# RMSNorm and matmul on one core: three more loads of sixteen tiles, squares nearer to their use, first casts in pieces

## Chip, core and metric

The kernel runs on one core of a Trainium2 chip. The metric is the device time of one execution in microseconds; the kernel before takes 209.28 us, the median of 7 runs (208.76 to 209.69). The engines of the core are named PE (matmul), ACT (ScalarE), DVE (VectorE), POOL (GpSimd) and SP (SyncE, which here only issues transfers). Sixteen DMA engines move the data.

## The reference

```python
batch, seq, dim, out_dim = 16, 1024, 512, 768
def reference(x, gamma, weight, eps):
    rms = np.sqrt(np.mean(x ** 2, axis=-1, keepdims=True) + eps)
    x_norm = x / rms * gamma
    return np.matmul(x_norm, weight).astype(np.float32)
```

All arrays are float32. There are 16,384 rows of x (33.5 MB), and as many rows of 768 results (50.3 MB).

## The kernel before

A tile is 128 rows of x; there are NT = 128 tiles, and NP = 64 pairs of tiles. The division by the rms is a scaling of a row, so it is done after the matmul, when a tile's sums leave PSUM; gamma is multiplied into the weights once, at the start.

**A tile's way.** A load brings rows of x into `xt`, two buffers of XG = 16 tiles. POOL casts them to bf16 (`cast`, L184 and L187). PE transposes a tile in two words of 128x128 float32, each of which holds two bf16 numbers (`transpose_word`, L225 and L229), and DVE copies the result from PSUM to `xT` (`evac`, L234 and L238). The last four tiles of each later group of sixteen go another way: POOL casts them at once into `xq` (`cast_quad`, L256 and L259), and DVE transposes 32x32 blocks, 16 instructions for a quad, three a turn (`move_quad`, L272, issued at L270). Then PE multiplies, four steps of 128 features, each with 512 and with 256 columns of the weights (`matmuls`, L305, instructions at L299), into one of three accumulators in PSUM. The even tile of a pair is scaled out of PSUM by ACT (L278), the odd one by DVE (L280), into `ot`. SP stores eight tiles at a time (L292), fewer at the start and the end.

**The scale.** ACT squares a tile and sums along the row in one instruction (`square`, L191 and L195, into `ssq`); `root` (L198) takes the root for several tiles on ACT (L200, into `rms`) and the reciprocal on DVE (L202, into `rstd`). For pairs 0 to 4 the squares and roots stand one pair ahead (`norms`). Pairs from 5 on follow the tables `NORM_GROUPS` and `norm_turns` (L211 to L213): in turn j the squares of pair j + 4 from turn 7 on, catching up in turns 5 and 6 with two pairs each, and a root for four pairs at a time, which stands with its reciprocal ahead of the turn's matmuls.

**Loads.** `x_first` and `x_size` (L137) say how tiles are loaded: group 0 in stretches of 2, 2, 4 and 8 tiles, groups 1, 5, 6 and 7 in two of 8, groups 2, 3 and 4 in one of 16. Within a group from 1 on, partition p holds sixteen neighbouring rows, so a load of 16 tiles moves 32 KB a partition in one piece, and one of 8 moves 16 KB. `load_until` (L180, called at L405) issues the loads of a group in turns 7, 15, 23 and so on: group g + 2 goes into the buffer of group g, and waits until all squares and casts that read the cells it overwrites are done. Groups 0 and 1 are loaded ahead of everything.

**The order of work** is written out by hand. The loop at L404 runs over the pairs j; one round is called a turn here. A turn lists, in this order: loads, casts (L406 to L411), quad cast or moves, squares and roots (L416 to L419), and then the matmuls of tiles 2j and 2j + 1. Between their steps `feeder` (L324) puts the transposes of pair j + 2, if it isn't of a quad. `Order.emit` then gives every engine its own instructions in that order, with a wait only where data or a buffer needs it. Each engine works through its list in order, and so does SP: a store that waits for its tiles holds up the load behind it.

The casts of a later group stand so: tiles 0 to 7 of it in turn 8g - 4 (one cast of eight), tiles 8 to 11 in turn 8g - 2, tiles 12 to 15 in turn 8g - 1 (the quad). Pair 8g, the first of a group, is transposed in turn 8g - 2.

Of the kernel before, what the change touches and what calls it, by code (L numbers as in the profile page):

```python
# [100 lines left out]
def kernel(  # L101
# [9 lines left out]
    PE, DVE, ACT, POOL, SP = nc.tensor, nc.vector, nc.scalar, nc.gpsimd, nc.sync  # L111
    order = Order(tc)

    def run(engine, issue, reads=(), writes=()):
        order.add(1, engine, issue, reads, writes)

    x = x.flatten_outer_dims()
    out = out.flatten_outer_dims()
# [4 lines left out]
    NP = NT // 2  # L123
    XG, OG = 16, 8
    AHEAD = 20

    def stretches(group, parts):
        first, size, i = {}, {}, 0
        for g in range(NT // group):
            for n in parts.get(g, [group]):  # L130
                for t in range(i, i + n):
                    first[t], size[t] = i, n
                i += n
        return first, size

    last = NT // OG - 1
    x_first, x_size = stretches(XG, {0: [2, 2, 4, 8], **{g: [8, 8] for g in (1, 5, 6, 7)}})  # L137
    o_first, o_size = stretches(OG, {0: [1, 1, 2, 4], last - 1: [4, 4], last: [4, 2, 2]})

    def rows(ap, i, n):  # L140
# [3 lines left out]
    def sb(name, shape, dtype):  # L144
        return nc.alloc_sbuf_tensor(name, shape, dtype).ap()
# [16 lines left out]
    rms = sb("rms", [P, NT], F32)  # L162
    rstd = sb("rstd", [P, NT], F32)
# [4 lines left out]
    def cells(name, slot, i, n=1):  # L168
        return [(name, slot, t) for t in range(i, i + n)]

    def x_of(i, n=1):
        return xt[i // XG % 2][:, i % XG:i % XG + n, :], cells("x", i // XG % 2, i % XG, n)
# [7 lines left out]
    def load_until(i):  # L180
        while starts and starts[0] < i:
            load(starts.pop(0))

    def cast(i, n=1):  # L184
        src, of = x_of(i, n)
        s = i // 8 % 2
        run(POOL, lambda: POOL.tensor_copy(out=xb[s][:, i % 8:i % 8 + n, :], in_=src), of, cells("xb", s, i % 8, n))  # L187
# [3 lines left out]
    def square(i):  # L191
        src, of = x_of(i)
        j = squares[0] % 2
        squares[0] += 1
        run(ACT, lambda: ACT.activation(out=jk[j], in_=src[:, 0, :], func=AF.Square, accum_out=ssq[:, i:i + 1]),  # L195
            of, [("jk", j), ("ssq", i)])

    def root(i, n):  # L198
        s = slice(i, i + n)
        run(ACT, lambda: ACT.activation(out=rms[:, s], in_=ssq[:, s], func=AF.Sqrt, scale=1.0 / D, bias=eps_sb),  # L200
            [("ssq", t) for t in range(i, i + n)] + ["eps"], [("rms", i)])
        run(DVE, lambda: DVE.reciprocal(out=rstd[:, s], in_=rms[:, s]), [("rms", i)],  # L202
            [("rstd", t) for t in range(i, i + n)])

    def norms(i, n):
        for t in range(n):
            square(i + t)
        root(i, n)


    NORM_GROUPS = [(5, 2), (7, 4)] + [(f, 4) for f in range(11, NP - 5, 4)] + [(NP - 5, 5)]  # L211
    norm_end = {f + s - 1: (2 * f, 2 * s) for f, s in NORM_GROUPS}
    norm_turns = {3: [5], 4: [6], 5: [7, 8], 6: [9, 10], **{j: [j + 4] for j in range(7, NP - 6)}, NP - 6: [NP - 2, NP - 1]}  # L213

    def norms_of_group(j):
        square(2 * j)
        square(2 * j + 1)
        if j in norm_end:
            root(*norm_end[j])

    def bank(j, t):

# [30 lines left out]
    def quad_of(j):  # L253
        return j // 2 if (2 * j) % XG >= XG - 4 and 2 * j >= XG else None

    def cast_quad(q):  # L256
        src, of = x_of(4 * q, 4)
        s = 4 * q // XG % 2
        run(POOL, lambda: POOL.tensor_copy(out=xq[s], in_=src), of, [("xq", s)])  # L259
        for t in range(4):  # L260
            xT_of[4 * q + t] = (xTq[s][:, t], ("xTq", s))
        words = xq[s].rearrange("p t d -> p (t d)").bitcast(F32).rearrange("p (a w) -> p a w", w=P)
        turned = xTq[s].rearrange("p t h m c -> p (t h m c)").bitcast(F32).rearrange("p (a m) -> p a m", m=P)
        for tokens in range(0, P, B):
            for features in range(0, P, B):
                quad_moves.append((turned[features:features + B, :, tokens:tokens + B],
                                   words[tokens:tokens + B, :, features:features + B], s))
# [4 lines left out]
    def move_quad(n):  # L272
        for _ in range(min(n, len(quad_moves))):
            move(*quad_moves.pop(0))

    def scale(engine, dst, src, r, reads, writes):
        if engine is ACT:
            run(ACT, lambda: ACT.mul(out=dst, in_=src, mul=r), reads, writes)  # L278
        else:
            run(DVE, lambda: DVE.tensor_single_scalar(out=dst, in_=src, scalar=r, op=mybir.AluOpType.mult), reads, writes)  # L280
# [3 lines left out]
    def accumulator():  # L284
        return next(turns) % 3

    def store(i):
        first, n = o_first[i], o_size[i]
        s = first // OG % 3
        if i == first + n - 1:  # L290
            src = ot[s][:, first % OG:first % OG + n, :]
            order.transfer(SP, lambda: SP.dma_start(out=rows(out, first, n), in_=src), reads=cells("ot", s, first % OG, n))  # L292
# [12 lines left out]
    def matmuls(i, a, ks, feed=None):  # L305
        block, cell = xT_of[i]
        for k in ks:
            lhsT = block[:, k // 2, :, k % 2]
            hold(lhsT, cell)
            for half, lo, hi in ((0, 0, WIDE), (1, WIDE, O)):  # L310
                product(ops[a][:, lo:hi], lhsT, w_bf[:, k, lo:hi], k == 0, k == K - 1,
                        [cell, ("w", k, half)], [("ops", a, half)])
            if feed:
                feed()

    def finish_tile(i, a, engine):
        s = i // OG % 3

        before = [("ot", s, i % OG - 1)] if i == o_first[i] + o_size[i] - 1 else []
        scale(engine, ot[s][:, i % OG, :], ops[a][:, :O], rstd[:, i:i + 1],  # L320
              [("ops", a, 0), ("ops", a, 1), ("rstd", i)] + before, [("ot", s, i % OG)])
        store(i)

    def feeder(pairs, gaps, alone=False):  # L324
        queue = [(j, t, h) for j in pairs for t in range(2) for h in range(2)]
        calls = iter(gaps)

        def feed():
            for _ in range(next(calls)):
                j, t, h = queue.pop(0)  # L330
                transpose_word(j, t, h)
                if alone and h == 1:
                    evac(j, t, 1)
                elif (t, h) == (1, 1):
                    evac(j)
        return feed
# [67 lines left out]
    for j in range(1, NP):  # L404
        load_until((2 * j + AHEAD + XG - 1) // XG * XG)  # L405
        if j in (1, 2):  # L406
            cast(4 * j + 4, 4)
        elif j % 8 == 4 and j + 4 < NP:
            cast(2 * j + 8, 8)
        elif j % 8 == 6 and j + 2 < NP:  # L410
            cast(2 * j + 12, 4)  # L411
        if (2 * j + 2) % XG == 0 and 2 * j + 2 < NT:
            cast_quad((2 * j + 2 + XG - 4) // 4)
        elif 2 * j >= XG:
            move_quad(3)
        if j < 4:  # L416
            norms(2 * j + 2, 2)
        for pair in norm_turns.get(j, []):
            norms_of_group(pair)  # L419
        if j < 3:  # L420
            feed = feeder([j + 1], mid if j == 1 else one, alone=j == 1)
        elif j == 3:
            feed = feeder([4, 5], both)
        elif j + 2 < NP and quad_of(j + 2) is None:
            feed = feeder([j + 2], two)
        else:
            feed = None
        for i, engine in ((2 * j, ACT), (2 * j + 1, DVE)):
            a = accumulator()
            matmuls(i, a, range(K), feed)  # L430
            finish_tile(i, a, engine)


    with tc.tile_critical():  # L434
# [45 lines left out]
```

## Time and profile before

| | |
|---|---|
| median of 7 runs | 209.28 us (208.76 to 209.69) |
| the profiled execution: its time, its span | 209.27 us, 207.5 us |
| PE busy | 192.8 us, 93% |
| DVE busy | 149.3 us, 72% |
| ACT busy | 144.5 us, 70% |
| POOL busy | 59.8 us, 29% |
| the DMA queue of loads and stores | 85.46 MB, 97.3% of the time of 16 engines |
| matmuls of tiles (L299), mean | 325 ns |
| transposes (L229), mean | 274 ns |
| squares (L195), 128 of them, mean | 619 ns |
| roots (L200), 20 of them, mean | 300 ns |
| reciprocals (L202), 20 of them, mean | 192 ns |
| cast of 8 tiles | 3.60 us |
| cast of 4 tiles | 1.89 us |
| cast of 2 tiles | 1.04 us |
| load of 16 tiles, issue to landing, median of 3 | 22.1 us |
| load of 8 tiles, issue to landing, median of 9 | 21.6 us |

The span runs from the first to the last instruction of one profiled execution; the time of that execution is 1.8 us longer. Busy time counts the instructions' own durations, without waits. PE overlaps its instructions, so its share says more than it is used. A load's time to landing holds the time that it waits behind earlier transfers.

### The profile page before, as it was taken

How to read it: one execution, taken by the hardware profiler on the slowest of the kernel's cores; microseconds unless marked ns; L12 is line 12 of the kernel's file. 1: busy time of each engine (PE TensorE's matmuls, PEld its weight loads, DVE VectorE, ACT ScalarE, POOL GpSimd, SP SyncE). 2: the span in 40 equal slices, each digit the busy share in tenths (PEclk: the TensorE clock that was granted, in tenths of full speed). 3: DMA queues.
4: the chain of work that ended last, by engine and by line, in shares of the span. 5: the costliest groups of instructions: out<-in, count | busy, mean ns of one | idle time of the engine just before them, and what ended most of it. 6: DMA issues, size and time to landing. Idle time of an engine off the chain costs nothing.

```text
span 207.5 us, 2761 instructions
## 1 busy us (share of the span) xinstructions
PE 192.8 (93%) x1212; PEld 72.3 (35%) x717; DVE 149.3 (72%) x255; ACT 144.5 (70%) x343; POOL 59.8 (29%) x34
## 2 busy tenths in 40 slices
PE   7789999999999999999999999999999999999910
PEld 1234444433334334432443334343334333432300
DVE  0455647998589957998579966999579975999310
ACT  4698897777768596856877686777777687763300
POOL 3247651019200390006700670006600373000000
PEclk9999999999999999999999999999999999999995
DMA  6999999999999999999999999999999999999992
GB/s 244 419 434 436 347 398 451 423 422 441 426 434 455 393 434 450 420 426 433 420 426 423 423 445 425 415 431 428 444 425 407 441 433 449 417 426 419 424 406 91
DMA packets 5632, 85.62 MB, mean 413 GB/s; under 512 B 626, under 2 KB 628, under 8 KB 1780
## 3 DMA queue, kind: packets, MB, share of 16 engines
q1 hardware_dynamic: 5616, 85.46, 97.3%
q8 instruction: 7, 0.11, 0.2%
q14 instruction: 5, 0.04, 0.0%
q10 hardware_dynamic: 4, 0.00, 0.0%
HBM read 35.13 MB, written 50.33 MB: 412 GB/s over the span
## 4 chain that ended last, share of the span: by engine, by line
PE 71%; DMA 16%; DVE 5%; issue 2%; SPq 1%; ACT 1%; POOL 1%; ACTq 0%
PE ps L299 62%; DMA xt<-in_x_dram 16%; PE ps L229 8%; DVE ot L280 2%; DVE xTq L270 2%; DVE xT L238 1%; POOL xb L187 1%; ACT jk L195 0%; SPq L344 0%; SPq L176 0%; ACT ot L278 0%; SPq L292 0%; DVE rstd L202 0%; SPq L475 0%; ACTq L93 0%
## 5 line engine op out<-in xcount | busy, mean ns | idle before, releaser
L299 PE MATMUL ps<-w_bf,xT 128*128 128x256 bf16 (+1 forms) x783 | 145.0, 325 | 2.3 <-DVE w_bf L280 1.0
L278 ACT ACTIVATE ot<-ps,rstd 128x768 f32<-128x768 f32 x64 | 57.5, 898 | 42.7 <-PE ps L299 41.1
L195 ACT ACTIVATE jk<-xt 128x512 bf16<-128x512 f32 x128 | 78.8, 619 | 6.7 <-DMA xt<-in_x_dram 6.6
L187 POOL CAST xb<-xt 128x2048 bf16<-128x2048 f32 (+3 forms) x21 | 46.2, 2218 | 112.2 <-DMA xt<-in_x_dram 107.9
L280 DVE TENSOR_SCALAR ot<-ps,rstd 128x768 f32<-128x768 f32 x64 | 64.8, 1013 | 8.9 <-PE ps L299 8.2
L295 PEld LDWEIGHTS <-xT 128*128 128x128 bf16 x400 | 39.2, 98 | 60.0 <-issue 51.9
L229 PE MATMUL ps<-ident_f,xb 128*128 128x128 f32 x200 | 53.9, 274 | 0.9 <-POOL xb L187 0.9
L238 DVE COPY xT<-ps 128x1024 bf16<-128x1024 bf16 (+1 forms) x53 | 34.5, 653 | 24.6 <-PE ps L229 22.9
L270 DVE STREAM_TRANSPOSE xTq<-xq 32x256 f32<-32x256 f32 x112 | 48.7, 435 | 3.4
L229 PEld LDWEIGHTS ps<-ident_f,xb 128*128 128x128 f32 x200 | 28.1, 142 | 46.3 <-issue 43.2
L299 PE MATMUL ps<-w_bf,xTq 128*128 128x256 bf16 (+1 forms) x217 | 41.8, 324 | 0.4
L195 ACT ACTIVATION_READ_ACCUMULATOR jk<-xt 128x1 f32 x128 | 24.3, 190 | 0.0
L295 PEld LDWEIGHTS <-xTq 128*128 128x128 bf16 x112 | 10.9, 98 | 14.5 <-issue 14.5
L259 POOL CAST xq<-xt 128x2048 bf16<-128x2048 f32 x7 | 13.3, 1893 | 0.0
L202 DVE RECIPROCAL rstd<-rms 128x8 f32<-128x8 f32 (+3 forms) x20 | 3.8, 192 | 7.5 <-ACT rms L200 7.3
L200 ACT ACTIVATE rms<-ssq,eps_sb 128x8 f32<-128x8 f32 (+3 forms) x20 | 6.0, 300 | 0.6
L299 PE MATMUL ps<-warm 128*128 128x512 bf16 x10 | 4.3, 571 | 1.4 <-DVE eps_sb L353 1.4
L278 ACT ACTIVATE w_bf<-w_f,g_sb 128x768 bf16<-128x768 f32 x2 | 1.9, 935 | 1.4 <-DMA w_f<-in_weight_dram 1.4
L376 DVE COPY g_sb<-ps 128x4 f32<-128x4 f32 x1 | 0.2, 162 | 3.2 <-PE ps L370 3.2
L340 ACT ACT_TABLE_LOAD x1 | 1.3, 1283 | 1.5 <-SPq L434 1.5
L280 DVE TENSOR_SCALAR w_bf<-w_f,g_sb 128x512 bf16<-128x512 f32 (+2 forms) x3 | 1.4, 482 | 0.8 <-DMA w_f<-in_weight_dram 0.8
L370 PEld LDWEIGHTS ps<-ident_f,g_row 2*128 2x128 f32 x2 | 0.3, 201 | 2.6 <-issue 2.6
(10 smaller groups left out, 1.9 us busy)
## 6 DMA issues: line engine op xcount, KB each, us to landing
out_dram<-ot SPq DMA_DIRECT2D x13, 3072.0 KB, 17.1
xt<-in_x_dram SPq DMA_DIRECT2D x9, 2048.0 KB, 21.6
xt<-in_x_dram SPq DMA_DIRECT2D x3, 4096.0 KB, 22.1
out_dram<-ot SPq DMA_DIRECT2D x4, 1536.0 KB, 11.8
out_dram<-ot SPq DMA_DIRECT2D x3, 768.0 KB, 8.5
w_f<-in_weight_dram SPq DMA_DIRECT2D x2, 768.0 KB, 5.4
xt<-in_x_dram SPq DMA_DIRECT2D x2, 512.0 KB, 5.1
xt<-in_x_dram SPq DMA_DIRECT2D x1, 1024.0 KB, 9.0
```

The costliest lines, as they stand in the source:

```text
L187: run(POOL, lambda: POOL.tensor_copy(out=xb[s][:, i % 8:i % 8 + n, :], in_=src), of, cells("xb", s, i % 8, n))
L195: run(ACT, lambda: ACT.activation(out=jk[j], in_=src[:, 0, :], func=AF.Square, accum_out=ssq[:, i:i + 1]), of, [("jk", j), ("ssq", i)])
L200: run(ACT, lambda: ACT.activation(out=rms[:, s], in_=ssq[:, s], func=AF.Sqrt, scale=1.0 / D, bias=eps_sb), [("ssq", t) for t in range(i, i ...
L202: run(DVE, lambda: DVE.reciprocal(out=rstd[:, s], in_=rms[:, s]), [("rms", i)], [("rstd", t) for t in range(i, i + n)])
L229: run(PE, lambda: PE.transpose(out=tp[b][:, t, h, :], in_=words[:, lo:lo + P], identity=ident_f), cells("xb", s, j % 4 * 2 + t) + ["ident" ...
L238: run(DVE, lambda: DVE.tensor_copy(out=dst[:, t:t + n, :], in_=src[:, t:t + n, :]), [("tp", b)], cells("xT", j % 4, t, n))
L259: run(POOL, lambda: POOL.tensor_copy(out=xq[s], in_=src), of, [("xq", s)])
L270: run(DVE, lambda: DVE.transpose(out=dst, in_=src), [("xq", s)], [("xTq", s)])
L278: run(ACT, lambda: ACT.mul(out=dst, in_=src, mul=r), reads, writes)
L280: run(DVE, lambda: DVE.tensor_single_scalar(out=dst, in_=src, scalar=r, op=mybir.AluOpType.mult), reads, writes)
L295: run(PE, lambda: PE.ldweights(lhsT), [cell])
L299: run(PE, lambda: PE.add_instruction(mybir.InstMatmult(name=nc.get_next_instruction_name(), engine=mybir.EngineType.PE, ins=[PE.lower_ap(r ...
```

## The change

- Groups 1, 5 and 6 (tiles 16 to 31 and 80 to 111) are loaded in one transfer of 4 MB each instead of two of 2 MB. Group 7 keeps its two halves.
- The tables of squares and roots go. In turn j, from 3 on, the squares of pair j + 2 are taken, and in every odd turn the root for two pairs (four tiles): pairs j + 1 and j + 2. Turn 3 takes one for pair 5 alone. Where a turn's squares read a tile of a new group, that is in turn 8g - 2 instead of 8g - 4.
- The reciprocal of such a root is put at the end of its turn on DVE, after the scale of tile 2j + 1; it used to stand ahead of the turn's matmuls.
- The cast of eight tiles in turn 8g - 4 becomes three: two, two and four tiles.

```diff
--- before.py
+++ after.py
@@ -134,7 +134,7 @@
         return first, size
 
     last = NT // OG - 1
-    x_first, x_size = stretches(XG, {0: [2, 2, 4, 8], **{g: [8, 8] for g in (1, 5, 6, 7)}})
+    x_first, x_size = stretches(XG, {0: [2, 2, 4, 8], **{g: [8, 8] for g in (7,)}})
     o_first, o_size = stretches(OG, {0: [1, 1, 2, 4], last - 1: [4, 4], last: [4, 2, 2]})
 
     def rows(ap, i, n):
@@ -195,12 +195,15 @@
         run(ACT, lambda: ACT.activation(out=jk[j], in_=src[:, 0, :], func=AF.Square, accum_out=ssq[:, i:i + 1]),
             of, [("jk", j), ("ssq", i)])
 
-    def root(i, n):
+    def root(i, n, later=None):
         s = slice(i, i + n)
         run(ACT, lambda: ACT.activation(out=rms[:, s], in_=ssq[:, s], func=AF.Sqrt, scale=1.0 / D, bias=eps_sb),
             [("ssq", t) for t in range(i, i + n)] + ["eps"], [("rms", i)])
-        run(DVE, lambda: DVE.reciprocal(out=rstd[:, s], in_=rms[:, s]), [("rms", i)],
-            [("rstd", t) for t in range(i, i + n)])
+
+        def invert():
+            run(DVE, lambda: DVE.reciprocal(out=rstd[:, s], in_=rms[:, s]), [("rms", i)],
+                [("rstd", t) for t in range(i, i + n)])
+        invert() if later is None else later.append(invert)
 
     def norms(i, n):
         for t in range(n):
@@ -208,15 +211,13 @@
         root(i, n)
 
 
-    NORM_GROUPS = [(5, 2), (7, 4)] + [(f, 4) for f in range(11, NP - 5, 4)] + [(NP - 5, 5)]
-    norm_end = {f + s - 1: (2 * f, 2 * s) for f, s in NORM_GROUPS}
-    norm_turns = {3: [5], 4: [6], 5: [7, 8], 6: [9, 10], **{j: [j + 4] for j in range(7, NP - 6)}, NP - 6: [NP - 2, NP - 1]}
-
-    def norms_of_group(j):
+    def norms_of_pair(j, later):
         square(2 * j)
         square(2 * j + 1)
-        if j in norm_end:
-            root(*norm_end[j])
+        if j == 5:
+            root(10, 2, later)
+        elif j % 2 == 1:
+            root(2 * j - 2, 4, later)
 
     def bank(j, t):
 
@@ -406,7 +407,9 @@
         if j in (1, 2):
             cast(4 * j + 4, 4)
         elif j % 8 == 4 and j + 4 < NP:
-            cast(2 * j + 8, 8)
+            cast(2 * j + 8, 2)
+            cast(2 * j + 10, 2)
+            cast(2 * j + 12, 4)
         elif j % 8 == 6 and j + 2 < NP:
             cast(2 * j + 12, 4)
         if (2 * j + 2) % XG == 0 and 2 * j + 2 < NT:
@@ -415,8 +418,9 @@
             move_quad(3)
         if j < 4:
             norms(2 * j + 2, 2)
-        for pair in norm_turns.get(j, []):
-            norms_of_group(pair)
+        later = []
+        if 3 <= j < NP - 2:
+            norms_of_pair(j + 2, later)
         if j < 3:
             feed = feeder([j + 1], mid if j == 1 else one, alone=j == 1)
         elif j == 3:
@@ -429,6 +433,8 @@
             a = accumulator()
             matmuls(i, a, range(K), feed)
             finish_tile(i, a, engine)
+        for invert in later:
+            invert()
 
 
     with tc.tile_critical():
```

## The prediction

> **What bounds the kernel now.** I read the page's slices first, then its DMA queues, then the windows, the waits of the SP queue, and last the timelines of PE, GpSimd and SP around the places the change touches. The slices (forty equal parts of the span; tenths busy):
>
> ```profile
> PE   7789999999999999999999999999999999999910
> DMA  6999999999999999999999999999999999999992
> GB/s 244 419 434 436 347 398 451 423 422 441 426 434 455 393 434 450 420 426 433 420 426 423 423 445 425 415 431 428 444 425 407 441 433 449 417 426 419 424 406 91
> ```
>
> Two resources look full at once. The windows of 23.5 us, one group of sixteen tiles each (columns: window, length, busy time of PE, weight loads, DVE, ACT, POOL with counts, clock, DMA share, GB/s), say the same in the middle of the run:
>
> ```profile
> 50.00:73.50 23.50, 23.34 (x151) 8.92 (x89) 19.15 (x33) 17.05 (x41) 5.92 (x3) 1.00 1.00 427
> 144.00:167.50 23.50, 23.34 (x151) 8.87 (x88) 19.16 (x33) 17.45 (x42) 6.90 (x3) 1.00 1.00 427
> ```
>
> Which one sets the end is read from the tail. Part 3 of the page and the end of the timeline:
>
> ```profile
> q1 hardware_dynamic: 5616, 85.46, 97.3%
> q8 instruction: 7, 0.11, 0.2%
> ```
> ```profile
> 196.21 3.20 SPq L292 DMA_DIRECT2D out_dram<-ot  x2
> 197.77 1.02 DVE L280 TENSOR_SCALAR ot<-ps,rstd 128x768 f32<-128x768 f32 x1 [1.58 <-PE ps L299]
> ```
> ```profile
> SPq L475 <- DMA out_dram<-ot: 7.1, 1, 7.1
> ```
>
> PE is done at 197.74, the last scale at 198.79, the last store is issued by 199.41, and then SP waits 7.1 us for it. That store is 768 KB, 1.8 us of work at 427 GB/s; the rest is queue. The records of single DMA packets make it plain: the fastest of the sixteen engines finishes its last packet at 202.2, the slowest at 206.1, and the slowest runs 6 KB packets back to back (234 ns each) right up to there. So the end is the slowest DMA engine's total work, and that engine would reach the last store's eight packets (8 x 0.234 = 1.9 us) only at about 204.2, while the store's data first move at 200.3. PE and everything behind it has some 3.9 us to spare. The lead of the fastest engine over the slowest grows from 0.6 us at 21 us to 3.5 us at 144 us.
>
> **What the Trainium skill says.** "DMA: Bandwidth & Descriptors", section on queues, rings and completion order: every DMA is split over up to sixteen engines and each consumes its ring in order; the section on the semaphore's 16 adds that a transfer has landed only when every engine has posted. The trace agrees: for tiles 88 to 95 the engines finish between 116.62 and 119.77, and the load counts as landed at 120.12. Its section on bandwidth gives 425 GB/s for a 16 MB load and a ceiling of 435; the windows show 427. "Runtime: NRT & Kernel Launch", section on instruction fetch, says that instructions are refilled by DMA in 16 KiB blocks, at a cost mostly hidden. The trace has seven such packets on queue 8, nearly 1 us each; with engines that are never idle, each delays the engine that carries it.
>
> **The change, part by part.**
>
> *Loads.* Three pairs of 2 MB loads become three 4 MB loads: 256 packets of 16 KB become 128 of 32 KB per group. Median packet durations are 611 ns and 1213 ns, so a merged pair saves 2 x 611 - 1213 = 9 ns. Each engine carries 8 per group: 8 x 9 = 72 ns, and one completion write of 9 ns; over three groups 3 x 81 = 0.24 us. Measured over whole groups it is less: the fastest engine takes 9.73, 9.75 and 9.78 us for groups 5, 6 and 7 (halves), and 9.80, 9.69 and 9.73 us for groups 2, 3 and 4 (whole), 9.75 against 9.74. Bounds 0 and -0.24; I take -0.15.
>
> *The same, for PE.* Tile 16's transposes can start only when all sixteen tiles have landed. GpSimd and PE before:
>
> ```profile
> 21.75 3.60 POOL L187 CAST xb<-xt 128x4096 bf16<-128x4096 f32 x1 [1.23 <-DMA xt<-in_x_dram]
> 28.31 1.89 POOL L187 CAST xb<-xt 128x2048 bf16<-128x2048 f32 x1 [2.96 <-PE ps L299]
> ```
> ```profile
> 28.34 0.27 PE L229 MATMUL ps<-ident_f,xb 128*128 128x128 f32 x1
> ```
>
> The second cast starts when the second half has landed (28.19 by its semaphore; "PE" as releaser is misread). The new cast of two tiles takes 1.04 us (the 128x1024 row at 9.39 us), so tiles 16 and 17 are ready at 29.35 and PE, which had transposed the first at 28.34 (turn j=6), stalls about 1.1 us. Pair 9's cast ends at 30.4, before its turn at 31.4 plus the stall. Had the cast stayed at eight tiles, the stall would have been 3.6; the split removes 2.56. For group 5 the whole load lands at 120.12; its cast ends at 121.3, and PE's first transposition there is at 122.43: covered. Group 6: 144.83, 146.0, and 145.85 plus the 1.1 already lost: covered. PE ends about 198.6 + (0 to 0.5), inside the 3.9 us. Without that cover the price is the full 1.1.
>
> *Who waits for a late PE.* Stores. The tightest place, in SP's timeline:
>
> ```profile
> 35.61 12.85 SPq L292 DMA_DIRECT2D out_dram<-ot  x2
> 48.50 0.89 SPq L176 DMA_DIRECT2D xt<-in_x_dram  x1
> ```
>
> The store of tiles 16 to 23 is issued at about 48.46 and its data could move 1.5 us later, as the last store's did, near 50.0. The rings drain at 51.12 (fastest) to 52.67 (slowest engine). A 1.1 us later store just meets the fastest engine and leaves the slowest 1.5 us. Later the queue is deeper (3.4 us at 71.9, 4.3 at 95.3).
>
> *Squares two pairs ahead.* They no longer hold ScalarE for a load (6.6 us in 5 waits) ahead of a scale, which had cost PE 0.25 us at 97.4. The price is that a buffer comes free later: group 3's load needs tile 31's squares, now at j=13 instead of 11, so about 52.3 (53.4 with the stall) instead of 48.50, and the stores are queued behind it on SP. But that load's data start at 58.39, behind the two stores, so 5 us of cover hide it; the covers of later groups are 10 to 14 us less these 4.
>
> *Roots.* 20 become 35: 15 x 0.30 = 4.5 us more on ScalarE and 15 x 0.19 = 2.9 us on DVE. ScalarE needs 2.1 to 2.3 us of a 3.04 us turn. DVE is tight where moves and evacuations meet: turns of 3.17 us against 3.04, a lag of 0.37 us after four; two reciprocals make it about 0.5 to 0.6, and the two turns without evacuations recover it. PE has three accumulators and so nearly 2 us before it feels a late scale. The reciprocal at the end of a turn waits for no root any more (7.3 us of DVE waits went there). Cost at the end: 0.
>
> *Casts.* 3.60 becomes 1.04 + 1.04 + 1.89 = 3.97 us, seven times: 2.6 us on an engine that idles 148 us. Nothing.
>
> *Instructions.* Some 44 more compute instructions may bring one more 8 KB fetch (309 ns), perhaps on the slowest engine: 0 to +0.3. I take 0.
>
> **Sum** against the profiled execution (209.27, span 207.5, so 1.8 outside; it is the median to 0.01): -0.15 for packets, 0 for the rest: 209.1.
>
> **Rivals.** *The dip goes away (faster).* In the loading of tiles 24 to 31, packets that start between 23.7 and 26.2 us take up to 1.2 us instead of 0.61; all sixteen engines lose 1.08 us there (5.97 us for the half against 4.89). It is the 347 in the slices. The trace doesn't show its cause. For its going: it falls into a load that the change replaces. Against: the second halves of groups 5, 6 and 7 have it not (4.86 us and the like), so halving alone doesn't make it. If it goes, tile 16 also lands 1.1 us earlier and PE hardly stalls: 209.28 - 0.15 - 1.08 = 208.1.
>
> *Tile 16 comes too late (slower).* The one mechanism that I see for a loss: PE's stall at j=6 delays the store of tiles 16 to 23 until the slowest engine has drained. It decides from a stall of 2.7 us (52.67 - 50.0), that is a landing after 29.8 instead of 28.19; beyond it every microsecond counts fully. A landing at 31.0 gives 209.1 + 1.2 = 210.3. For it: engine spread and dip vary; against: 1.6 us are needed first.
>
> *The kernel is bound by PE after all.* Then the 1.1 us stall less the 0.25 shows in full: 210.0. The 7.1 us wait at the end speaks against it.
>
> **Numbers.** A change under 0.2% (0.42 us) can't be told from none here. Forecast 0.40 (0.30 within, 0.07 faster, 0.03 slower); dip gone 0.30; late tile or PE bound 0.18; anything else 0.12 (0.05 faster, 0.02 within, 0.05 slower). Faster 0.42, same 0.32, slower 0.26. The likeliest's own range is 208.8 to 209.5; the whole reaches from 207.9 (dip gone) to 210.1 (PE bound).
>
> **What would show it.** Right: 32 KB packets near 1213 ns in groups 1 to 6, a single PE wait of about 1.1 us on the cast at 28 us, none at 122 or 146, the last packet of the slowest engine within 0.4 us of 206.1, ScalarE's waits for loads gone. Wrong: DMA share below 0.98 in any middle window, a slowest engine that ends with gaps between its last packets, PE idle above 3 us in all, or a slice near 25 us at over 400 GB/s (the dip gone).

## The result and the profile after

The changed kernel is slower: 210.69 us, the median of 15 runs (209.64 to 212.75), against 209.16 us (36 runs) for the kernel before, a ratio of 1.0074 with a 95% interval of 1.0056 to 1.0091. That is 1.5 us. Ratios here and below compare fast runs alone; runs more than 1.5% above the fastest of their kernel are left out, which matters for e4 only. The execution that was profiled first took 210.01 us and is one of the quicker ones; a second profile, of an execution of 211.30 us, stands with the experiments. Both are needed.

The slices of the page of the changed kernel, first profile:

```profile
PE   7789979999999999999999999999999999999920
DMA  6999989999999899999999999999999999999992
GB/s 243 419 438 450 368 352 450 441 416 430 430 436 460 369 424 428 471 386 435 424 457 420 416 435 420 441 447 391 435 414 419 433 443 443 411 435 416 406 415 96
```

The dip in slices five and six (368 and 352 GB/s) is still there, and the DMA row is full as before. The same windows as before (window, length, busy time of PE, weight loads, DVE, ACT, POOL, clock, DMA share, GB/s) show that only the first differs, and little, 421 against 427:

```profile
50.00:73.50 23.50, 23.34 (x151) 8.88 (x88) 19.15 (x36) 18.13 (x45) 5.42 (x5) 1.00 1.00 421
144.00:167.50 23.50, 23.21 (x149) 8.73 (x87) 18.82 (x35) 17.77 (x45) 9.62 (x8) 1.00 1.00 429
```

Part 3 of the page, the same bytes in fewer packets, and the tail: DVE's and SP's timeline, and SP's wait for the last store.

```profile
q1 hardware_dynamic: 5184, 85.46, 97.3%
q8 instruction: 7, 0.11, 0.2%
```
```profile
199.07 1.02 DVE L281 TENSOR_SCALAR ot<-ps,rstd 128x768 f32<-128x768 f32 x1 [1.58 <-PE ps L300]
```
```profile
197.52 3.20 SPq L293 DMA_DIRECT2D out_dram<-ot  x2
```
```profile
SPq L481 <- DMA out_dram<-ot: 5.9, 1, 5.9
```

PE, and with it the last scale, is 1.3 us later than before, and the wait for the last store is 1.2 us shorter: most of PE's loss is absorbed, as predicted. In this execution the last DMA packet ends at 206.38 us instead of 206.11. Yet the span grew from 207.49 to 208.08 us, so 0.32 us arose behind the last packet; that is taken up below.

The place of the change, GpSimd, PE and SP:

```profile
28.55 5.70 POOL L187 CAST xb<-xt 128x1024 bf16<-128x1024 f32 x4 [7.96 <-DMA xt<-in_x_dram]
```
```profile
29.64 0.33 PE L230 MATMUL ps<-ident_f,xb 128*128 128x128 f32 x1 [1.07 <-POOL xb L187]
```
```profile
49.48 0.33 SPq L293 DMA_DIRECT2D out_dram<-ot  x1
51.77 0.34 SPq L176 DMA_DIRECT2D xt<-in_x_dram  x1
60.39 0.33 SPq L293 DMA_DIRECT2D out_dram<-ot  x1
```

PE waits 1.07 us for tile 16's cast, the store of tiles 16 to 23 is issued at 49.48 instead of 48.12, group 3's load at 51.77 instead of 48.50, the next store at 60.39 instead of 59.03. The stall and the delay of the first store were forecast within 0.3 us; the load was forecast at 53.4. What was wrong is what the delay costs.

### The profile page after: what moved, and what is told of

Same layout as the page of the kernel before. It is cut to its first block, busy times and chain, and to the rows that moved or that the text cites. A ratio compares the mean times of both kernels' runs of the same rounds, so it can differ in the third digit from the quotient of the medians.

```text
span 208.1 us, 2795 instructions
## 1 busy us (share of the span) xinstructions
PE 193.4 (93%) x1212; PEld 72.6 (35%) x717; DVE 149.6 (72%) x270; ACT 148.7 (71%) x358; POOL 61.5 (30%) x48
## 4 chain that ended last, share of the span: by engine, by line
PE 68%; DMA 23%; SPq 1%; issue 1%; ACT 1%; POOL 1%; DVE 0%; POOLq 0%
PE ps L300 60%; DMA xt<-in_x_dram 23%; PE ps L230 8%; POOL xb L187 1%; SPq L176 1%; ACT jk L195 1%; DVE ot L281 0%; ACT ot L279 0%; SPq L345 0%; SPq L481 0%; POOLq L93 0%; SPq L440 0%
## 5 line engine op out<-in xcount | busy, mean ns | idle before, releaser
L187 POOL CAST xb<-xt 128x1024 bf16<-128x1024 f32 (+2 forms) x35 | 47.9, 1406 | 111.6 <-DMA xt<-in_x_dram 111.6
L200 ACT ACTIVATE rms<-ssq,eps_sb 128x4 f32<-128x4 f32 (+1 forms) x35 | 10.4, 297 | 1.1
L204 DVE RECIPROCAL rstd<-rms 128x4 f32<-128x4 f32 (+1 forms) x35 | 5.8, 167 | 4.2 <-ACT rms L200 4.2
```

## Experiments

Three theories stand at the start. A: PE's stall on tile 16 costs. B: whole loads of sixteen tiles are slower for the DMA engines. C: something in the tail, behind the last packet. Theories D and E, and A' (the late PE costs in some other way than through the issue of its stores), are formed on the way.

**Which part of the change.** Only the groups that are loaded in halves differ:

```diff
# e1, from the changed kernel
-    ... for g in (7,)}})
+    ... for g in (1, 7)}})
# e2: (5, 6, 7)    e3: (1, 5, 6, 7)
# e4, from the kernel before
-    ... for g in (1, 5, 6, 7)}})
+    ... for g in (7,)}})
```

> The changed kernel with group 1 (tiles 16 to 31) loaded in two halves again. Theory A (the 1.1 us stall of PE on the whole first group is what costs): the stall at 28 to 30 us goes, PE ends near 197.8 instead of 199.1, and the time falls to 209.2 +- 0.4. Theory B (loads of 16 tiles are slower for the DMA engines, each of the three takes its part): only a third of the 1.5 us comes back, 210.2. Theory C (the tail: in the changed kernel's profile the last drain of GpSimd ends 0.47 us later than before although the last store lands only 0.14 us later; more GpSimd instructions): that 0.45 us stays, 209.6 to 209.7 if A holds for the rest.

> The changed kernel with groups 5 and 6 (tiles 80 to 111) in halves again, group 1 whole. A: no gain, 210.7 (the small PE wait of 0.3 us at 147 us goes, behind the stall already lost). B: two thirds come back, 209.7. C: 210.7, the GpSimd tail stays.

> The changed kernel with the loads of before: squares, roots and casts alone are new. A: 209.2, as before, PE without a stall. B: 209.2. C: 209.6 to 209.7, with the late GpSimd drain in the profile's tail.

> The kernel before with the three whole loads alone; squares four pairs ahead, casts of eight. A: tile 16's cast of eight ends 3.6 us after the landing, PE stalls about 3.6 us at 28 us and ScalarE waits for loads at 120 and 145 us: 212.5 to 214. B: 210.7. C: no GpSimd tail, so 0.45 less than what A or B say.

Ratios to the kernel before on the same chip: e1 1.0033 (1.0019 to 1.0046), 209.58 us; e2 1.0068 (1.0047 to 1.0089), 210.44; e3 1.0011 (1.0001 to 1.0020), 209.23; e4 1.0221 (1.0174 to 1.0268), from three of its six runs, which scatter from 211.89 to 216.37. So the new squares, roots and casts cost 0.1%. Group 1 as a whole makes 0.4 to 0.6% (changed kernel less e1, e2 less e3), groups 5 and 6 at most 0.2% (e1 less e3). Without the new casts and squares, e4, the whole loads cost 2.2% or more: the casts in pieces and the later squares together take most of that back. A is favoured for group 1, since B would put two thirds on groups 5 and 6. Theory C expected the late end of GpSimd in e2 and e3 too; both profiles lack it, for a reason that the tail shows below.

**The late tile without the whole load.** From e3, with loads in halves, GpSimd copies unneeded numbers ahead of tile 16's cast:

```diff
         elif j % 8 == 4 and j + 4 < NP:
+            if j == 4:
+                for width in [2048] * 4 + [512]:    # e6: * 5, e7: * 6
+                    busy(width)      # a copy of so many weights to bf16
             cast(2 * j + 8, 2)
```

> The changed squares, roots and casts with the loads of before (halves), and in front of tile 16's cast GpSimd copies unneeded numbers (four times 1.84 us and 0.52 us), so that the cast starts near 28.4 us as in the changed kernel, though its load landed at 21.6. PE should stall 1.0 to 1.1 us at 28 us. Theory A (the late tile, and nothing else, makes group 1's part of the loss): 0.3 to 0.5% above the same kernel without the delay, 210.0 to 210.2. Theory B (the whole load itself slows the DMA engines): no loss, 209.3. Theory D (the stall is free up to some 3 us, and only executions whose landing is later than in the profile pay): 209.3 too, and a narrow spread.

> The same with one more copy of 1.84 us: a stall of 2.9 us at PE. A: two to three times the loss of the shorter delay, 211 or more. B: 209.3. D: at the edge, 209.4 to 210.5.

> One more copy, a stall of 4.7 us. A and D: 1.84 us more than with the delay before it (the slope is one by then). B: still 209.3; that is excluded if the stall passes the 3.7 us between PE's end and the DMA's end.

Measured: e5 210.23 us, 1.0059 (1.0039 to 1.0078); e6 213.59, 1.0231; e7 216.20, 1.0344. The stall of 1.46 us in e5's profile costs 1.0 us against e3, with loads in halves: A holds for group 1, B falls. D falls too: the stall is not free up to 3 us. And the slope is more than one, where A and D expected one for e7. From e5 to e6 the stall grows by 1.96 us (1.46 to 3.42) and the time by 3.4, from e6 to e7 by 2.0 and 2.6.

**A second profile of the changed kernel.**

> The changed kernel itself once more, for another profile: its first one was a run of 210.01, below its median of 210.69. A and D: an execution near 210.7 has a later landing of group 1 and a PE stall above the 1.4 us of the first profile. B: the same stall, and more DMA time per packet. C: the late GpSimd drain again, in every profile.

The runs had a median of 210.42 us; the profiled one took 211.30. Its GpSimd and PE timelines:

```profile
29.59 5.71 POOL L187 CAST xb<-xt 128x1024 bf16<-128x1024 f32 x4 [8.88 <-DMA xt<-in_x_dram]
```
```profile
30.69 0.33 PE L230 MATMUL ps<-ident_f,xb 128*128 128x128 f32 x1 [2.00 <-POOL xb L187]
```

Group 1 landed 1.0 us later than in the first profile, and PE waits 2.0 us. The same late landing, with a first cast at 29.6, shows in two more profiles of kernels that load group 1 whole (e10 and e11); the early one, with a first cast at 28.55 and 28.59, in the first profile and in e2. All sixteen DMA engines must post, and one alone is late: in the first profile fifteen have posted by 27.75 us and the last at 28.42, in the second fifteen by 27.63 and the last at 29.46. The packet records show what stands there. They name no engine, but the times fit to a few ns: in the second profile one engine's last data packet ends at 27.45 us, a 16 KB instruction packet of queue 8 follows at once and takes 0.93 us, and only then comes that engine's completion write, at 28.39. In e10 and e11 it is the same. In the first profile and in e2 the instruction packet starts at 24.6 and 25.2 us, ahead of the engine's last data packet.

The store of tiles 16 to 23 is now issued at 50.52 us, and the next one at 61.43. The windows of the second profile around the ends of the two transfers concerned, that store and the load of group 3 behind it,

```profile
57.00:60.00 3.00, 3.00 (x22) 1.22 (x12) 1.58 (x3) 2.38 (x7) 0.00 (x0) 1.00 1.11 374
66.00:71.00 5.00, 5.00 (x36) 2.03 (x20) 4.80 (x9) 3.47 (x11) 0.00 (x0) 1.00 0.90 321
```

and those of the kernel before:

```profile
57.00:60.00 3.00, 3.00 (x21) 1.18 (x12) 2.54 (x5) 2.08 (x6) 0.00 (x0) 1.00 1.09 467
66.00:71.00 5.00, 4.95 (x34) 1.91 (x19) 4.77 (x10) 2.64 (x7) 0.28 (x1) 1.00 0.93 393
```

The last two columns are the reading. A packet counts in the window in which it starts, so a short window can show a share above 1. The DMA engines are about as busy as before (1.11 and 0.90 against 1.09 and 0.93), but they move 374 and 321 GB/s instead of 467 and 393. They don't run dry there; their packets take longer. The packet records say it singly: 28 packets of 32 KB that start between 66.9 and 68.7 us take 1.35 times their usual 1.21 us in the mean, and up to 2.6 us.

**What makes them slow?** Theory E: a transfer that is issued late into the one that is running. First a load alone, in the kernel before:

```diff
# e9; e12 takes ("ot", 0, 5), the scale of tile 29
+        late = [("ssq", 37)] if i == 48 else []
-        order.transfer(SP, lambda: SP.dma_start(...), writes=to)
+        order.transfer(SP, lambda: SP.dma_start(...), reads=late, writes=to)
```

> The kernel before, in which only the load of group 3 (tiles 48 to 63) waits in SP's queue for the squares of tile 37, so that it is issued near 55.8 us instead of 48.5; PE, the casts and all other issues stay. At 55.8 us the only transfer left in the queue is the running store of tiles 16 to 23, which ends at 58.4. Theory E (an issue that finds only the running transfer in the queue makes the last packets of that transfer slow, 0.3 to 0.4 of their time over some 2.5 us, on all sixteen engines): a slow stretch at 56.5 to 58.5 us, and 209.7 to 210.2. Theory A' (it is the late PE itself that costs, through the end of the run): 209.2 and no slow stretch there.

> The kernel before, in which only the load of group 3 waits on SP for the scale of tile 29, so that it is issued near 56.0 us, some 5 us after the store ahead of it has begun to move and 2.5 us before that store ends. The run with an issue at 52.6 us cost nothing. Theory E (a transfer that is issued late into the one running makes the last packets of that one slow): a slow stretch of about 2 us at 56.5 to 58.5, 209.7 to 210.1. If not: 209.1, the lateness of a load alone is free as long as the queue does not run dry.

e9's issue came at 52.59 us, earlier than meant, since ScalarE takes those squares sooner than I had read; it cost nothing: 1.0010 (0.9992 to 1.0028). e12's came at 56.17: 1.0013 (1.0004 to 1.0021). A late load is nearly free, and E in that form falls: from 57 to 60 us e12 loses 0.2 us per engine instead of some 0.7 to 1, and its time is not 209.7. But e12 is not without slow packets. At the end of the late load itself its window shows

```profile
66.00:71.00 5.00, 5.00 (x34) 1.85 (x19) 4.77 (x10) 2.51 (x6) 0.00 (x0) 1.00 0.99 360
```

against 393 GB/s in the kernel before, 0.7 us lost on each engine near 67 us, with both stores on time. Then stores, again in the kernel before, with PE left alone:

```diff
# e13: moved = {31: 33}     e14: moved = {23: 25, 31: 33}
-        store(i)
+        if i not in moved:
+            store(i)
+        for tile, after in moved.items():
+            if after == i:
+                store(tile)      # its transfer also reads tile `after`
```

> The kernel before, in which only the store of tiles 24 to 31 is issued after the scale of tile 33, near 62.1 us instead of 59.0 (in the changed kernel: 60.4 and 61.4). PE and everything else stay. Theory E: the load of group 3, which runs from 58.4 to 68, gets slow packets at 66 to 68, all engines lose 0.7 to 1 us, 209.7 to 210.1. Theory A' (the late PE costs in some other way than through the issue of its stores): 209.1.

> The kernel before with two stores issued late, as a stall of PE would make them: tiles 16 to 23 after the scale of tile 25 (near 50.6 us instead of 48.1), tiles 24 to 31 after that of tile 33 (62.1). PE has no stall. Theory E: slow stretches near 58 and 67 us, together 1.5 us and more on all engines, 210.2 to 211, as with the stall. A': 209.1.

e13 (tiles 24 to 31 stored at 62.2 us): 1.0001 (0.9989 to 1.0012), nothing. e14: 210.62 us, 1.0075 (1.0060 to 1.0090). Two late stores, with every cast, square and matmul as in the kernel before, give a loss as large as the changed kernel's. They are later than there (50.74 us against 49.48 and 50.52 in its two profiles, 62.22 against 60.39 and 61.43), so this shows what late stores can do, not the exact share. Group 3's load goes out behind the first of them at 51.12 us; e9 delays it further and costs nothing. SP's timeline and the windows of e14:

```profile
35.77 15.31 SPq L293 DMA_DIRECT2D out_dram<-ot  x2
51.12 0.58 SPq L176 DMA_DIRECT2D xt<-in_x_dram  x1
62.22 9.81 SPq L293 DMA_DIRECT2D out_dram<-ot  x2
```
```profile
57.00:60.00 3.00, 3.00 (x22) 1.22 (x12) 2.39 (x4) 2.09 (x6) 0.00 (x0) 1.00 1.23 415
66.00:71.00 5.00, 5.00 (x34) 1.83 (x19) 4.77 (x10) 2.48 (x6) 0.00 (x0) 1.00 0.97 336
```

Since the store of tiles 24 to 31 alone is free, the one of tiles 16 to 23 is needed for the loss; it was not tried alone. When it is issued, one transfer is left in the queue, the store of tiles 8 to 15. The margin in the table is the time from the issue to the moment when the fastest engine has finished that transfer: in e14 the issue stands at 50.74 us, and that engine ended at 50.80. "Lost" is the sum of all packets' durations over the median of their size, divided by 16 engines. Except for the last column, a row is one profiled execution:

| kernel | PE's wait near 28 us | store of 16 to 23 issued | margin to the fastest engine's end | lost, 40 to 80 us | lost, whole run | last packet ends | the profiled execution | median of the runs |
|---|---|---|---|---|---|---|---|---|
| before | 0 | 48.12 | 3.01 | 0.28 | 2.59 | 206.11 | 209.27 | 209.16 |
| e15 | 0 | 48.08 | 2.92 | 0.32 | 2.64 | 205.97 | 209.26 | 209.25 |
| e3 | 0 | 48.17 | 2.77 | 0.39 | 2.39 | 205.76 | 209.07 | 209.23 |
| e1 | 0 | 48.27 | 2.60 | 0.34 | 2.62 | 206.56 | 210.09 | 209.58 |
| e9 | 0 | 48.23 | 2.58 | 0.45 | 2.80 | 206.09 | 209.27 | 209.15 |
| e13 | 0 | 48.27 | 2.57 | 0.51 | 2.37 | 205.76 | 208.92 | 208.92 |
| e12 | 0 | 48.30 | 2.49 | 1.22 | 2.83 | 206.02 | 209.21 | 209.21 |
| after, first | 1.07 | 49.48 | 1.70 | 0.59 | 3.28 | 206.38 | 210.01 | 210.69 |
| e2 | 0.39 | 49.52 | 1.46 | 1.10 | 3.09 | 206.38 | 209.53 | 210.44 |
| e5 | 1.46 | 49.90 | 0.93 | 1.52 | 3.73 | 207.63 | 210.75 | 210.23 |
| e10 | 1.84 | 50.56 | 0.59 | 1.89 | 4.25 | 207.76 | 210.91 | 210.34 |
| after, second | 2.00 | 50.52 | 0.55 | 1.77 | 4.30 | 207.68 | 211.30 | 210.42 |
| e14 | 0 | 50.74 | 0.05 | 2.07 | 4.05 | 207.87 | 210.88 | 210.62 |

Over the whole run, 2 us more of slow packets go with a last packet some 2 us later, give or take half a microsecond. From 40 to 80 us the loss grows, by and large, as the margin falls, with e12 as the exception. (PE reaches tile 16 in e2 0.7 us later than in the changed kernel's first profile, so its wait is shorter at nearly the same issue.) With 2.5 us and more the times are those of the kernel before, but for e1, whose tail is taken up below; with less than 1 us they are not. No profile lies between 1.70 and 2.49, so where the loss begins is known only that far, and e12 says that the margin of this store is not the whole condition.

Nor does the loss need a dry queue. Counted from the packet records near 51 us, an engine stands without a packet for 0.06 us in the mean or less in all these profiles but e14, where it is 0.35. In e6, with a margin of -2.67, the queue does run dry, for 2.8 us; the window then shows it in the DMA share, 0.55, where e14 has 0.93 and the others 0.99 and more:

```profile
50.00:57.00 7.00, 7.00 (x45) 2.25 (x23) 6.15 (x12) 5.47 (x13) 3.74 (x2) 1.00 0.55 232
```

**More depth instead.** In the changed kernel tiles 16 to 31 are stored by four, so that the first halves leave earlier:

```diff
-    ... {0: [1, 1, 2, 4], last - 1: [4, 4], last: [4, 2, 2]})
+    ... {0: [1, 1, 2, 4], 2: [4, 4], 3: [4, 4], last - 1: [4, 4], last: [4, 2, 2]})
```

> The changed kernel, in which tiles 16 to 23 and 24 to 31 are stored in two transfers of four tiles each, so that the first half of each is issued some 6 us earlier: the PE stall stays, but an issue no longer finds the queue with one transfer alone. Theory E: the slow stretches near 58 and 68 us go, 209.5 to 209.9. Theory A': no change, 210.4 to 210.7.

```profile
57.00:60.00 3.00, 3.00 (x22) 1.22 (x12) 1.58 (x3) 2.38 (x8) 0.00 (x0) 1.00 1.03 438
66.00:71.00 5.00, 5.00 (x35) 2.04 (x21) 4.80 (x9) 3.47 (x11) 0.00 (x0) 1.00 1.07 446
92.00:95.00 3.00, 2.95 (x21) 1.18 (x13) 2.87 (x6) 2.46 (x8) 0.00 (x0) 1.00 0.81 289
```

The slow stretches at 58 and 68 us are gone (438 and 446 GB/s), but a new one stands at 92 to 95, at the end of group 4's load; the same window has 371 in the first profile of the changed kernel. The time is 210.53, 1.0065 (1.0043 to 1.0087), no gain. So E's 209.5 to 209.9 was wrong, though its two stretches went. That the DMA, no longer held up at 60 us, gets ahead and meets the stores of the late PE one group later is a reading, not shown; in this profile 1.0 us is also lost in the first 6 us of the run, against 0.2 to 0.8 in the others.

**The tail.** Twelve small memsets on GpSimd at the start, in the changed kernel (e10) and in e1 (e15):

```diff
     run(POOL, lambda: POOL.memset(ident_f, 0.0), [], ["ident"])
+    for _ in range(12):
+        run(POOL, lambda: POOL.memset(xq[1][:, 0, :1], 0.0), [], [("xq", 1)])
```

> The changed kernel with twelve small memsets more on GpSimd at the start, where it idles. Theory C (the pause of 0.34 us of GpSimd among the last semaphores comes from where its program crosses a block of instructions): the pause leaves the last 2 us of the span, 210.3 to 210.4 against the 210.4 to 210.7 of the changed kernel. If it depends on something else, it stays, and so does the time.

> The changed kernel with group 1 in halves (209.58 before) and the twelve memsets more on GpSimd at the start. If groups 5 and 6 as whole loads cost nothing and the 0.35 us over the same kernel with all halves (209.23) are GpSimd's pause at the end: no pause, 209.2. If the whole loads of groups 5 and 6 cost through the PE wait of 1.5 us seen at 147 us: 209.5 to 209.6.

From the end of the last packet to the end of the span pass 1.38 us in the kernel before, 1.70 and 1.71 in the two profiles of the changed kernel, 1.64 in e1, 1.84 in e11; 1.22 in e10 and 1.38 in e15. The difference is one pause of GpSimd, about 0.34 us longer than the usual step between two of its last instructions; the memsets remove it from the tail. e10: 210.34 us, 1.0057 (1.0030 to 1.0084), 0.1 to 0.35 us under the changed kernel, which this comparison can hardly tell from nothing. e15: 209.25 us, 1.0009 (0.9995 to 1.0023), against e1's 1.0033: here it is clearer, and with it the 0.2% that e1 had left for groups 5 and 6. Their whole loads cost nothing that can be told from the interval, though PE waits 0.6 us near 146 us in e15 and 1.5 us in e1.

The pause belongs to a place in GpSimd's program. In the changed kernel's two profiles, in e1, e11 and e3 it stands ahead of the 69th recorded instruction of GpSimd. The changed kernel has 73 of them, e1 74, so the pause falls behind the last store. e3, with 76, has it at 196.3 us, ten microseconds before that store ends, and the 69th of e2's 75 is itself the one that waits for the end; so e2 and e3, with the same fourteen instructions more, have tails of 1.24 and 1.38 us. The kernel before has 62. Why the pause stands there is open. The thought behind the memsets was that the next instructions have to be fetched there, since instructions come in blocks, by DMA ("Runtime: NRT & Kernel Launch" of the Trainium skill, instruction fetch mechanics). The records fit only in part: in the changed kernels whose tail has the pause they show five 8 KB instruction packets between 20 and 201 us, and in those without it a sixth; but e3's sixth comes at 198.8 us, after its pause.

## Why the prediction was wrong

**What bounds the kernel: right.** The end follows the slowest DMA engine. In the first profile PE's end moved by 1.3 us and the wait for the last store shrank by 1.2.

**Packets of merged loads: right.** The sum of the median durations fell from 199.34 to 199.09 us per engine, 0.25; 0.15 was taken and 0.24 was the bound. Groups 5 and 6 whole cost nothing that shows (e15).

**PE's stall: right in kind, mis-sized.** 1.1 us was forecast from a landing at 28.19; it was 1.07 in the first profile, from 28.42, and 2.0 in the second, from 29.46. The prediction took the landing of the halves as that of the whole, to 0.1 us. A landing is the slowest engine's, and it varied by a microsecond with the place of one instruction packet. The prediction had seen that these packets delay the engine that carries them, but gave it no price here. Group 6 was called covered; PE waited 1.5 us there in e1.

**"A 1.1 us later store just meets the fastest engine and leaves the slowest 1.5 us": this is the step that failed.** I let a store be free until the queue is empty, and every microsecond cost in full after that, from a stall of 2.7 us. The rival "tile 16 comes too late" named the right place and the right store, but with that threshold and 1.6 us of stall to spare it was rated unlikely. In its place: with a margin of 0.9 us and less, and a queue that is dry for 0.35 us at most, the DMA engines stay busy but slow, in that store and in the load behind it. They lost 1.2 to 1.8 us more there than in the kernel before, and the time rose by 1.0 us (e5 against e3) and 1.6 us (e14). In the changed kernel itself 0.3 us was lost at a stall of 1.07 us and 1.5 us at one of 2.0. Why the packets slow is open.

The 1.5 us from a store's issue to its first data was wrong as well, to the other side. It was read from the last store, but there no engine stood idle before 201.9 us, so that store's data waited for the stores ahead of it. Where the queue had run dry, data moved 0.8 us after the issue (e4, e6, e7). By the prediction's rule that would have made the late store safer still, so this slip did not cause the miss.

**Squares two pairs ahead: right.** Group 3's load was issued 3.3 us later and hidden; e9 and e12 delay it by 4 and 8 us for 0.1%. ScalarE's waits for loads fell from 6.6 to 2.5 us (3.8 in the second profile); they were expected to go.

**Roots and reciprocals: a miss without a price.** I saw the late reciprocal as covered. ScalarE waits for it seven times, as the waits of the changed kernel say (engine and line, releaser, total, times, longest):

```profile
ACT ot L279 <- DVE rstd L204: 7.1, 7, 1.0
```

PE doesn't wait on it, and e3, which has it, costs 0.1%.

**Casts: right for time, wrong as "nothing".** The split bought what it was costed at, but the fourteen instructions lengthened GpSimd's program, so that a pause of 0.34 us fell at its end. I had set the extra instructions at 0 to 0.3 us, on the DMA's side, and taken 0.

**The dip stays.** The rival that it goes was wrong: it is in every profile at 24 to 26 us, whole load or halves, though its size varies (between 20 and 40 us 1.34 and 1.22 us are lost per engine in the two profiles of the changed kernel, 1.14 before, 0.77 to 0.85 in e1 and e3, 0.49 in e2).

Sum, as estimates from these ratios, in parts of the loss of 0.74%: group 1's late stores 0.4 to 0.6, GpSimd's pause 0.15 to 0.2, the new squares, roots and casts otherwise about 0.1. No run beat the kernel before by more than its interval; e13, at 208.92 us, is the same.

## To carry to other kernels

In a kernel whose DMA queue is never empty, ask of each store how long before the queue's end it is issued, not whether the queue runs dry: here a margin of 2.5 to 3 us cost nothing, and one of 0.9 us or less cost 1.0 to 1.6 us. When a load is merged, its first tile comes at the pace of the slowest DMA engine, so take the spread of several executions into the price, not the landing of one. A comparison of kernels within half a per cent should look behind the last transfer too, where a pause of 0.3 us can come from instruction counts alone.

## What the runs showed of the hardware

- Most DMA packets of one size take the same time: 85 to 99% of those of 16, 24 and 32 KB lie within 3% of their medians (611, 912 and 1213 ns). But for stretches of about 2 us many of them, on nearly all sixteen engines, take 1.3 to 1.7 times as long in the mean: near 24 to 26 us in all profiles, near 58 us, near 68 us or both in the profiles whose store of tiles 16 to 23 was issued late, near 67 us in e12 behind a late load, near 92 us in e11. Apart from the first of these, they stand at the end of a transfer. A busy share of 1.0 doesn't show it; GB/s of a short window does. Why the engines slow is open. A late issue of the following load costs 0.1% at most (e9, e12), one of the second store nothing (e13).
- On a queue that had run dry, data moved 0.8 us after the issue (e4, e6, e7).
- DMA engines drift apart: their spread at the end of a load was 1.0 us at 27 us and 3.5 us at 144 us in the kernel before. The post of one engine can hold a load back: with a 16 KB instruction packet (0.88 to 0.93 us) between its last data packet and its completion write, group 1 landed 1.0 us later (second profile, e10, e11).
- The same pause stood ahead of GpSimd's 69th recorded instruction in five profiles; it was worth 0.34 us at the end of the span where that instruction came behind the last store.
